# A decoder block in one list schedule: from a schedule of its first phase to a schedule of the whole program

## The chip, the cores and the metric

The kernel runs on one core of one Trainium2 chip. The metric is device time in microseconds (us) of that core. Five engines work side by side, each through its own stream of instructions in a fixed order: PE (matmuls; its weight loads are listed as PEld), DVE, ACT and POOL (elementwise work), and SP, which here only issues DMA transfers.

## The reference

One decoder block on x of 1024 tokens by 1024 features, all in float32:

```python
xn = rmsnorm(h, norm_mix_g);  proj = xn @ w_in
att = forgetting_attention(q, k, v, log_sigmoid(f + b))      # 8 heads of 64, causal
gm  = chunked_spatial_gating(gelu(u), vg, ...)               # 8 groups of 64, chunks of 128 tokens
h = h + concat(att, gm) @ w_out
xn = rmsnorm(h, norm_ffn_g)
a, g = split(conv3(xn @ w_up))                               # 2 x 2816 columns, causal conv of width 3
h = h + (silu(g) * a) @ w_down
out = rmsnorm(h, norm_final_g)
```

## The kernel before

The large products are done in float32 precision from a pair of reduced-precision terms: each operand x is split into a high part (rounded to fp32r) and a low part (x minus the high part), and a product is three matmuls, high by high, high by low, low by high. `split_w` (L387) does that for weights: ACT casts the high part (L390), DVE subtracts for the low part (L396). Around this, each large product is a Strassen-like scheme with seven block products in place of eight; POOL forms the sums of weight blocks (L1342 to L1345 for the FFN), DVE the sums of inputs.

The stages follow each other on PE: the projection (from L335 on, `tmul` L487 to L493, `product` L630 to L635, and `qk_step` L845, which makes one unit of queries and keys, split into high and low parts and written to DRAM through `emit` (L790, DMAs at L797); L887 empties the last bank of a unit into the second half of a tile `G` whose first half such a DMA is still reading); the attention, head by head (`Head`, L982: logits L1007/L1008, transposes L1028, the weighted sum of values L1047), with the spatial gating in between; w_out (`wmm`, L1362 to L1366, accumulating four groups G0 to G3 into one PSUM bank), the second norm (`norm2`, L1376 to L1386), and `flip` (L1390 to L1418), which transposes the normed tokens (L1400) and splits them into `xB`/`xT` operands; the FFN's up projection, 22 units; and the down projection (L1650) with the final norm.

One unit of the up projection (`up_a`, `up_b`, L1487 to L1565) is seven products of 12 matmuls of 128x512 each, into banks named `b` and `s`. DVE empties the banks: `u` (L1517, L1521), and `h` in parts (L1527, L1529, L1545). The last product of a unit accumulates onto the bank that L1527 reads, so it waits for L1527. Then the convolution runs on DVE (L1505 and L1507 on tiles `cg` and `ca`), the gate (L1548), and, once in two units, four sums `hs` (L1559 to L1562), which go to DRAM as `hx` and come back in the down projection as `sg`. For later units, weights are loaded (`raw<-wup`, on SP), summed by POOL into `sg`, and split by ACT and DVE into `wha` (two blocks per unit, straight from `raw`) and `whb` (five blocks).

The order is set in two ways. Class `Pace` (L33) records the instructions from `pace.start()` (L305) to `pace.settle()` (L1288), that is the projection, the attention and the gating. `settle` (L150) builds the dependencies of these, gives each a due time (backwards from PE's order: the due time of a successor less the instruction's own latency and a hop), and lets `run` (L226) issue them in a simulated machine, on each engine the ready one that is due first; the order that results is pinned on each engine. It runs up to three rounds and keeps the best. What stands in the program after L1288 (w_out, norm2, flip, the whole FFN) is not recorded. It keeps the tile framework's order, and by hand a few instructions are held behind others: `behind` (L400) holds weight splits behind the sums of `flip(7)` (key "sums") or behind a unit's L1527 (key "hg").

Of the kernel before, what the change touches and what calls it, by code (L numbers as in the profile page):

```python
# [10 lines left out]
BF16 = mybir.dt.bfloat16  # L11
# [21 lines left out]
class Pace:  # L33
# [3 lines left out]
    def __init__(self, tc):  # L37
        self.tc, self.slot, self.ring, self.prev, self.held = tc, {}, {}, {}, {}

    def keep(self, t, key):  # L40

        name = t.tensor.name if hasattr(t, "tensor") else t.name
        self.slot[name] = key
        self.prev[name] = self.held.get(key)
        self.held[key] = name

    def pool(self, p):
        pace = self

        class Paced:  # L50

            def tile(self, shape, dt, tag=None, bufs=None, name=None, **kw):
                if tag is None:
                    t = p.tile(shape, dt, name=name, **kw)
                    pace.keep(t, (id(p), name))
                    return t
                n = pace.ring.get((id(p), tag), 0)
                pace.ring[id(p), tag] = n + 1
                b = bufs or 4
                tag = "%s.%d" % (tag, n % b) if b > 1 else tag  # L60
                t = p.tile(shape, dt, tag=tag, bufs=1, name=name, **kw)
                pace.keep(t, (id(p), tag))
                return t

            def release(self):
                p.release()

        return Paced()
# [4 lines left out]
    def view(self, a):  # L73
# [6 lines left out]
        if t.name in self.slot:  # L80
            if self.slot[t.name][0] in self.banks:
                return t.name, 0, P, 1, True
# [61 lines left out]

    def psum(self, a):
        return self.slot.get(a.bass_ap.tensor.name, (0, ""))[0] in self.banks

    banks = ()

    def settle(self, rounds=3):  # L150
# [4 lines left out]
        for i in list(self.tc.nc.cur_bb.bb.instructions)[self.first:]:  # L155
# [27 lines left out]
            ops.append((i, eng, c, deps, SET.get(str(getattr(i, "func", "")).split(".")[-1], 0) if eng == "ACT" else 0))  # L183
        for name, ks in opens.items():
            old = self.prev[name]
            while old is not None and old not in uses:
                old = self.prev[old]
            for k in ks if old is not None else ():
                ops[k][3].update(uses[old] - {k})
# [1603 lines left out]
```

## Time and profile before

| what | us |
|---|---|
| median of 3 runs | 1074.82 (1074.76 to 1074.94) |
| the profiled execution, its own time | 1075.99 |
| its span in the trace | 1074.3 |
| PE busy | 1053.2 (98%) |
| DVE busy | 905.7 (84%) |
| ACT busy | 574.8 (54%) |
| POOL busy | 238.9 (22%) |

The granted TensorE clock of the profiled execution was 0.995 of full speed on average. Two kinds of time are told apart below. Busy time counts an instruction from its start to its end; matmuls overlap one another, so PE is 98% busy without being at its peak. Lost time on PE is read from the gaps between the starts of its matmuls. The rows of an answer that lists instructions in time give the start in us from the span's beginning, the duration, the engine, the line, what is written and read, and, in brackets, the idle time before it and what ended it. Tiles are named as in the program, with buffer numbers left out.

### The profile page before, as it was taken

Reading aid. Unit: us, or ns where it says so; the run is one execution under the profiler, and the core shown is the slowest. Engines: PE = TensorE matmul, PEld = TensorE weight load, DVE = VectorE, ACT = ScalarE, POOL = GpSimd, SP = SyncE. Lnnn points to the kernel's source line nnn. Section 1 sums busy time; section 2 is a strip of 40 time slices with the busy share of each in tenths; the row PEclk is TensorE's granted clock in tenths of the full one; section 3 lists DMA queues with packets and bytes.
Section 4 is the critical chain, followed back from the end, with each engine's and each line's share of the span. In section 5 each row is a group of like instructions: output and inputs, shape, how many; then the busy total and the mean of one; then the engine's idle time right before and its main releaser. Section 6 shows DMA issues by size and latency. Waiting matters only on the chain.

```text
span 1074.3 us, 14284 instructions
## 1 busy us (share of the span) xinstructions
PE 1053.2 (98%) x4885; PEld 865.8 (81%) x4885; DVE 905.7 (84%) x1390; ACT 574.8 (54%) x1006; POOL 238.9 (22%) x211
## 2 busy tenths in 40 slices
PE   9999999999999999998999999999999999999997
PEld 6888778788888877876888888888888888888886
DVE  6986699898888868999899899998998776898774
ACT  6657445577776746753444444444344444454653
POOL 0002224232362250054233232233322000000000
PEclk9999999999999999999999999999999999999999
DMA  9243336886675354223323323232331998333442
GB/s 333 96 145 98 90 115 176 265 255 189 193 220 158 109 199 164 77 73 125 120 67 119 126 82 115 99 114 83 108 118 50 302 342 305 106 92 99 144 122 96
DMA packets 64712, 158.16 MB, mean 147 GB/s; under 512 B 7672, under 2 KB 7936, under 8 KB 64640
## 3 DMA queue, kind: packets, MB, share of 16 engines
q1 hardware_dynamic: 64352, 156.70, 44.8%
q8 instruction: 38, 0.62, 0.2%
q10 hardware_dynamic: 288, 0.56, 0.1%
q14 instruction: 34, 0.28, 0.1%
HBM read 114.95 MB, written 42.27 MB: 146 GB/s over the span
## 4 chain that ended last, share of the span: by engine, by line
PE 82%; issue 7%; DVE 5%; DMA 3%; POOL 2%; ACT 1%; SPq 0%; POOLq 0%; DVEq 0%; ACTq 0%
PE s L1455 20%; PE b L1455 14%; PE s L1650 11%; PE b L1650 8%; PE s L493 6%; PE b L493 5%; PE fl L1123 4%; PE po L1047 3%; PE tr L1028 3%; PE b L635 2%; PE s L635 2%; PE lg L1008 2%; PE lg L1007 2%; DMA qd<-G 1%; DMA x<-kd 1%
## 5 line engine op out<-in xcount | busy, mean ns | idle before, releaser
L1455 PE MATMUL s<-xT,whb 128*128 128x512 f32 x804 | 189.8, 389 | 0.2 <-DVE u L1517 0.2
L1455 PEld LDWEIGHTS s<-xT,whb 128*128 128x128 f32 x804 | 150.7, 188 | 32.0 <-DVE u L1517 0.6
L1455 PE MATMUL b<-xB,wha 128*128 128x512 f32 x528 | 127.2, 390 | 2.0 <-DVE wha L396 2.0
L1650 PE MATMUL s<-whb,wha 128*128 128x512 f32 x528 | 120.2, 389 | 0.0
L1455 PEld LDWEIGHTS b<-xB,wha 128*128 128x128 f32 x528 | 98.9, 188 | 22.8 <-DVE wha L396 2.4
L1650 PEld LDWEIGHTS s<-whb,wha 128*128 128x128 f32 x528 | 99.1, 188 | 20.7
L390 ACT CAST wha<-sg 128x512 fp32r<-128x512 f32 x77 | 48.0, 623 | 97.1 <-PE b L1650 46.0
L390 ACT CAST whb<-sg 128x512 fp32r<-128x512 f32 x82 | 50.6, 618 | 74.8 <-PE s L1455 67.1
L1650 PE MATMUL b<-whb,wha 128*128 128x512 f32 x396 | 90.2, 389 | 0.0
L396 DVE TENSOR_TENSOR wha<-sg,wha 128x512 fp32r<-128x512 f32 x77 | 53.0, 690 | 41.9 <-ACT wha L390 41.9
L1650 PEld LDWEIGHTS b<-whb,wha 128*128 128x128 f32 x396 | 74.3, 188 | 15.4
L1123 PE MATMUL fl<-whl,H 128*128 128x512 f32 x192 | 71.5, 416 | 0.0
L396 DVE TENSOR_TENSOR whb<-sg,whb 128x512 fp32r<-128x512 f32 x82 | 62.8, 767 | 9.0 <-ACT whb L390 8.7
L1455 PE MATMUL s<-xB,whb 128*128 128x512 f32 x264 | 64.9, 395 | 4.6 <-DVE h L1527 4.6
L1455 PEld LDWEIGHTS s<-xB,whb 128*128 128x128 f32 x264 | 50.4, 192 | 15.6 <-DVE h L1527 5.0
L1455 PE MATMUL b<-xT,whb 128*128 128x512 f32 x252 | 61.0, 389 | 0.0
L1342 POOL TENSOR_TENSOR sg<-raw 128x512 f32<-128x512 f32 x20 | 28.1, 1404 | 146.9 <-DVE whb L396 84.0
L1047 PE MATMUL po<-pt,V 128*128 128x512 f32 (+1 forms) x192 | 58.8, 364 | 1.0 <-DVE pt L1039 1.0
L1039 DVE TENSOR_TENSOR pt<-tr,pt 128x512 fp32r<-128x512 f32 (+2 forms) x96 | 51.9, 551 | 8.6 <-ACT pt L1034 8.1
L1034 ACT CAST pt<-tr 128x512 fp32r<-128x512 f32 (+3 forms) x96 | 45.4, 475 | 25.8 <-PE tr L1028 23.1
L1455 PEld LDWEIGHTS b<-xT,whb 128*128 128x128 f32 x252 | 47.2, 188 | 10.0 <-DVE whb L396 0.3
L1343 POOL TENSOR_TENSOR sg<-sg,raw 128x512 f32<-128x512 f32 x20 | 41.2, 2058 | 62.7 <-issue 62.6
(382 smaller groups left out, 2344.1 us busy)
## 6 DMA issues: line engine op xcount, KB each, us to landing
raw<-wup SPq DMA_DIRECT2D x44, 512.0 KB, 3.6
sg<-hx SPq DMA_DIRECT2D x77, 256.0 KB, 2.6
hx<-hs SPq DMA_DIRECT2D x44, 256.0 KB, 2.2
hx<-ca SPq DMA_DIRECT2D x33, 256.0 KB, 2.0
xT<-wdn SPq DMA_DIRECT2D x28, 256.0 KB, 4.8
raw<-wqk SPq DMA_DIRECT2D x8, 512.0 KB, 3.9
qd<-G SPq DMA_DIRECT2D x16, 256.0 KB, 9.3
kd<-G SPq DMA_DIRECT2D x16, 256.0 KB, 3.2
```

Source lines behind the costliest of these rows:

```text
L390: act.copy(h, src)
L396: return eng.tensor_tensor(out=l, in0=src, in1=f32(h), op=ALU.subtract)
L493: pe.matmul(banks[m], xs(n, xi, k)[:, ms], w[:, wi, :], start=(first and k == 0 and c == 0), stop=(k == 3 and c == 2), skip_group_check=True)
L635: pe.matmul(ps, w[:, wi, ks], xs(n, xi, k), start=(first and c == 0), stop=(c == 11), skip_group_check=True)
L1028: pe.transpose(ps[:, (q - 4 * hf) * P:(q - 4 * hf + 1) * P], self.t[q][:, k * P:(k + 1) * P], ident)
L1034: act.copy(pt[:, 0, o:512], ps[:, o:512])
L1039: dve.tensor_tensor(out=pt[:, 1, o:512], in0=ps[:, o:512], in1=f32(pt[:, 0, o:512]), op=ALU.subtract)
L1047: pe.matmul(self.po[hf][:, o:512], lhs, pt[:, s, o:512], start=(k == 0 and s == 0), stop=(k == 4 * hf + 3 and s == 1), skip_group_check=True)
L1123: pe.matmul(self.bank, sgT[k][:, xi, ts_], self.w[hf, k][:, wi, :], start=(k == 0 and i == 0), stop=(k == 3 and i == 2))
L1343: pool.tensor_tensor(out=s[1], in0=s[0], in1=a11, op=ALU.add)
L1455: pe.matmul(ps, w[:, wi, ks], xb[:, xi, k, :], start=(first and n == 0), stop=(n == 11), skip_group_check=True)
L1650: pe.matmul(banks[bk + m], xh[:, xi, ms], wh[:, wi, :], start=(first and p_ == 0 and n == 0), stop=(p_ == NP - 1 and n == 2), skip_group_c ...
```

## The change

It touches what the planner sees and how it weighs, and hardly what is computed. The instructions are the same in kind and number; only their order differs.

1. `pace.settle()` moves from L1288 to the end of the program, and the pools that came after it (`upl`, `xtp`, `upr`, `pst`, `dn`) are opened through `pace.pool`. So the schedule covers w_out, norm2, flip and the FFN too. The hand-set orders (`gates`, `behind`, `after`) go.
2. A place in SBUF is no longer followed by pool and tag but by bytes: each pool knows the pool under it on its side (`extent`), and `prior` finds for each tile the earlier tiles that lay on its bytes, whichever pool they came from. A pool that opens where another was released waits for all that used the released one ("TURN", an entry without time).
3. Reads of one PSUM bank by two engines are put in order.
4. The due time: for a predecessor on the same engine (SP excepted) the successor's due time is taken less the predecessor's pace, no longer less its latency and a hop. Matmuls that accumulate into one bank, 12 of them say, so become due close together.
5. SP issues at most 3000 ns of transfer time ahead of the modelled bus (`BACKLOG`).
6. `flip` of the first four token tiles writes, per bank, ACT's high part and ACT's copy one after the other, and DVE's low parts (`lo_of`) behind them.

```diff
@@ prior: which earlier tiles lay on a tile's bytes
+    def prior(self, uses):
+        now, prev = {"sb": [], "psum": []}, {}
+        for name in self.made:
+            pool, key = self.slot[name]
+            a, b = pool.extent(key)
+            old, keep = set(), []
+            for x, y, n in now[pool.space]:
+                if x < b and a < y:
+                    old.add(n)
...
+            prev[name] = set().union(*({n} if n in uses else prev[n] for n in old))
+        return prev
@@ settle
-                        if hit and (w or o[1]):
+                        if hit and (w or o[1] or self.bank(name) and ops[o[0]][1] != eng):
...
+        for p in {p: 0 for p, _ in self.slot.values()}:
+            if p.after:
+                ops.append((None, "TURN", (0, 0, 0), set().union(*(whose[q] for q in p.after)), 0))
+                for k in whose[p]:
+                    ops[k][3].add(len(ops) - 1)
...
                 for s in succ[k]:
-                    d = min(d, due[s] - o[2][1] - HOP)
+                    d = min(d, due[s] - (o[2][0] if ops[s][1] == o[1] != "SP" else o[2][1] + HOP))
@@ run
-                f = free[e]
+                f = max(free[e], bus - BACKLOG) if e == "SP" else free[e]
@@ block_kernel
     for hf in range(2):
         wo_split(3, hf, "pool")
-    pace.settle()
...
-    upl = tc.alloc_tile_pool(name="upl", bufs=1, reuse_waits="tile")
-    xtp = tc.alloc_tile_pool(name="xtp", bufs=1, reuse_waits="tile")
+    upl = pace.pool(tc.alloc_tile_pool(name="upl", bufs=1, reuse_waits="tile"))
+    xtp = pace.pool(tc.alloc_tile_pool(name="xtp", bufs=1, reuse_waits="tile"))
...
-                behind(split_w(wr[:, ("A11", "A12").index(n), :], (t[:, 0], t[:, 1])), "sums" if i < AHEAD else "hg")
+                split_w(wr[:, ("A11", "A12").index(n), :], (t[:, 0], t[:, 1]))
...
         if tt < 4:
             for n, p3 in (("B11", pp[0]), ("B21", pp[1])):
-                hl_of(n, c, p3)
+                act.copy(XB[n][:, 0, :, c], p3)
+                act.copy(xt[n][:, :, c], p3)
             for n, p3 in (("B11", pp[0]), ("B21", pp[1])):
-                act.copy(xt[n][:, :, c], p3)
+                lo_of(n, c, p3)
...
         finish(4 + m, hi)
+    pace.settle()
     dn.release()
```

The lines of the changed kernel have shifted: L396 is L441 there, L797 is L835, L815 to L817 are L853 to L855, L960 is L998, L1505 and L1507 are L1539 and L1541, L1517 is L1551, L1521 is L1555, L1527 is L1561, L1529 is L1563, L1545 is L1575, L1548 is L1578, L1559 to L1562 are L1589 to L1592, and L1575 is L1605.

How the order moves is shown at three places. In the rows, a number after a tile's name tells its instances apart, and is the same in both kernels.

The first is on DVE, in the first units of the up projection, where the weight block `wha_834` is split that PE needs for the first product of unit 3 (`b_836`). Before:

```order
L1521 TENSOR_TENSOR u_831_4761<-u_829_4746,s_830_4748 128x512
L1507 SCALAR_TENSOR_TENSOR ca_818_4706<-h_804_4611,cp_75,ca_818_4706 128x1022
L1527 TENSOR_TENSOR h_833_4776<-u_831_4761,s_832_4763 128x512
L1548 TENSOR_TENSOR ca_818_4706<-ca_818_4706,cg_816_4685 128x1024
L396 TENSOR_TENSOR whb_835_4806<-sg_826_4739,whb_835_4806 128x512
L396 TENSOR_TENSOR whb_841_4832<-sg_827_4740,whb_841_4832 128x512
L1529 TENSOR_TENSOR h_833_4776<-u_829_4746,s_830_4748 128x512
L396 TENSOR_TENSOR wha_834_4803<-raw_823_4734,wha_834_4803 128x512
L396 TENSOR_TENSOR wha_840_4829<-raw_823_4734,wha_840_4829 128x512
```

And now:

```order
L1563 TENSOR_TENSOR h_812_4663<-u_808_4633,s_809_4635 128x512
L441 TENSOR_TENSOR whb_821_4717<-raw_731_4062,whb_821_4717 128x512
L1605 TENSOR_TENSOR h_815_4682<-b_801_4578,u_814_4681 128x512
L441 TENSOR_TENSOR wha_862_4960<-raw_851_4878,wha_862_4960 128x512
L1575 TENSOR_TENSOR h_804_4611<-s_811_4650,u_808_4633 128x512
L441 TENSOR_TENSOR wha_834_4803<-raw_823_4734,wha_834_4803 128x512
L441 TENSOR_TENSOR wha_840_4829<-raw_823_4734,wha_840_4829 128x512
L1539 SCALAR_TENSOR_TENSOR cg_816_4685<-h_812_4663,cp_75,cg_816_4685 128x1023
L1551 TENSOR_TENSOR u_829_4746<-b_822_4721,u_814_4681 128x512
L1539 SCALAR_TENSOR_TENSOR ca_818_4706<-h_804_4611,cp_75,ca_818_4706 128x1023
```

The split of `wha_834` stood behind two convolution steps (`ca_818`), a gate and the emptying of `h_833`; it now stands ahead of all of these, directly behind `h_804` and `wha_862`, a block for unit 4 that was split 25 rows further down before.

The second place is on DVE some 15 rows later, at `h_861`, the emptying of the bank `s_860` for which the last product of unit 3 waits. Before:

```order
L1548 TENSOR_TENSOR ca_842_4837<-ca_842_4837,cg_839_4825 128x1024
L1521 TENSOR_TENSOR u_859_4905<-u_857_4890,s_858_4892 128x512
L1559 TENSOR_TENSOR hs_846_4853<-ca_818_4706,ca_842_4837 128x512
L396 TENSOR_TENSOR whb_863_4963<-sg_854_4883,whb_863_4963 128x512
L1560 TENSOR_TENSOR hs_847_4854<-hs_846_4853,ca_818_4706 128x512
L1561 TENSOR_TENSOR hs_848_4855<-ca_818_4706 128x512
L396 TENSOR_TENSOR whb_869_4989<-sg_855_4884,whb_869_4989 128x512
L396 TENSOR_TENSOR whb_871_4999<-sg_853_4882,whb_871_4999 128x512
L1562 TENSOR_TENSOR hs_849_4856<-hs_847_4854,ca_842_4837 128x512
L396 TENSOR_TENSOR wha_886_5092<-raw_875_5022,wha_886_5092 128x512
L1527 TENSOR_TENSOR h_861_4933<-u_859_4905,s_860_4920 128x512
```

And now:

```order
L1578 TENSOR_TENSOR ca_818_4706<-ca_818_4706,cg_816_4685 128x1024
L1551 TENSOR_TENSOR u_857_4890<-b_850_4865,u_837_4810 128x512
L1539 SCALAR_TENSOR_TENSOR ca_842_4837<-h_815_4682,cp_75,ca_842_4837 128x1023
L1555 TENSOR_TENSOR u_859_4905<-u_857_4890,s_858_4892 128x512
L1541 SCALAR_TENSOR_TENSOR ca_842_4837<-h_815_4682,cp_75,ca_842_4837 128x1022
L441 TENSOR_TENSOR whb_863_4963<-sg_854_4883,whb_863_4963 128x512
L1563 TENSOR_TENSOR h_833_4776<-u_829_4746,s_830_4748 128x512
L441 TENSOR_TENSOR whb_869_4989<-sg_855_4884,whb_869_4989 128x512
L441 TENSOR_TENSOR wha_868_4986<-raw_851_4878,wha_868_4986 128x512
L441 TENSOR_TENSOR whb_871_4999<-sg_853_4882,whb_871_4999 128x512
L1561 TENSOR_TENSOR h_861_4933<-u_859_4905,s_860_4920 128x512
```

The four sums `hs_846` to `hs_849`, the gate of `ca_842`, and the block `wha_886` (for unit 5) stood ahead of `h_861`, as did the convolution `cg_839`; now they come behind it, and `wha_868`, a block of unit 4, comes ahead of it.

The third place is on SP in the projection, at the DMAs around the write of one unit's results to DRAM (`qd<-G`, issued twice for a tile; L887 writes into the same tile `G` and starts when this transfer has ended). The rows `x<-qd`, `x<-kd`, `x<-ncd` load what the attention's first head reads, `pt<-vd` its values, `raw<-wv` weights. Before:

```order
L824 DMA raw_177_1610<-wv 128x1024
L824 DMA raw_176_1608<-wv 128x1024
L813 DMA x1_170_1551<-qd_112 128x1024
L814 DMA x1_170_1551<-kd_113 128x1024
L797 DMA qd_112<-G1_111_999 64x2x512 x2
L815 DMA x2_171_1552<-kd_113 64x1024
L816 DMA x2_171_1552<-kd_113 64x1024
L817 DMA x2_171_1552<-ncd_115 128x1024
L960 DMA pt_187_1659<-vd_116 128x1024
L797 DMA qd_112<-G1_111_999 64x2x512 x2
```

And now:

```order
L862 DMA raw_177_1610<-wv 128x1024
L851 DMA x1_170_1551<-qd_112 128x1024
L835 DMA qd_112<-G1_111_999 64x2x512 x2
L862 DMA raw_176_1608<-wv 128x1024
L852 DMA x1_170_1551<-kd_113 128x1024
L853 DMA x2_171_1552<-kd_113 64x1024
L835 DMA qd_112<-G1_111_999 64x2x512 x2
L854 DMA x2_171_1552<-kd_113 64x1024
L855 DMA x2_171_1552<-ncd_115 128x1024
L998 DMA pt_187_1659<-vd_116 128x1024
```

The last `qd<-G` of the rows before stood behind the rest of the `x2_171` loads (L816, L817) and behind `pt_187<-vd`; now it stands ahead of these three, and the earlier `qd<-G` has one of the two `raw<-wv` loads behind it that stood in front.

More of the change, by code (lines that the diff above doesn't have):

```diff
@@ L230, in run @@
         ready = [0.0] * n
-        can = {e: [] for e in ("PE", "DVE", "ACT", "POOL", "SP")}
+        can = {e: [] for e in ("PE", "DVE", "ACT", "POOL", "SP", "TURN")}
         free = dict.fromkeys(can, 0.0)
@@ L252, in run @@
             i, e, (cad, lat, x), deps, fn = ops[k]
+            turn = e == "TURN"
             can[e].remove(k)
@@ L278, in run @@
         return order, start, end
-SLACK = 30000.0
-LOOK = {"PE": 0.0, "DVE": 0.0, "ACT": 0.0, "POOL": 0.0, "SP": 0.0}
-def after(tc, later, earlier):
-    tc.add_manual_dep(later.ins, earlier.ins.name, mybir.DependencyInfo(
-        mybir.DependencyClass.NoSync, mybir.DependencyReason.DATA), reason="order")
+SLACK, BACKLOG = 30000.0, 3000.0
+LOOK = {"PE": 0.0, "DVE": 0.0, "ACT": 0.0, "POOL": 0.0, "SP": 0.0, "TURN": 0.0}
 @with_exitstack
@@ L1469, in block_kernel @@
         if i == 0:
-            last = flip(7)
+            flip(7)
             WB[0](("S2", "S3"))
-            gates["sums"] = last
     def late_sum(n, src):
```

121 lines of the change are left out of this document (70 added, 51 removed).

## The prediction

> **What bounds the kernel now.** I read the page first, then PE's waits, a table of stretches, and the instructions in time around each wait.
>
> The page's first lines:
>
> ```profile
> span 1074.3 us, 14284 instructions
> PE 1053.2 (98%) x4885; PEld 865.8 (81%) x4885; DVE 905.7 (84%) x1390; ACT 574.8 (54%) x1006; POOL 238.9 (22%) x211
> ```
>
> PE is the bound, so the change can only remove time in which PE stands still or runs at half pace. PE's waits, longest first (engine, bank and line, what ended the wait, us, times, longest):
>
> ```profile
> PE s L1455 <- DVE h L1527: 4.6, 1, 4.6
> PE b L1455 <- DVE wha L396: 2.0, 1, 2.0
> PE s L493 <- DVE G L887: 1.9, 1, 1.9
> PE b L635 <- ACT whl L390: 1.6, 1, 1.6
> ...
> PE po L1047 <- DVE pt L1039: 1.0, 1, 1.0
> PE s L1400 <- DVE pt L1374: 0.7, 1, 0.7
> PE s L749 <- DVE gg L748: 0.5, 1, 0.5
> ```
>
> Seven waits, 12.3 us in sum. That is nearly all there is to win: the stretches (us of each engine busy, with instruction counts; then PEclk, DMA share, GB/s) show where PE keeps its pace.
>
> ```profile
> 200.00:240.00 40.00, 38.13 (x191) 31.50 (x191) 35.45 (x80) 26.46 (x54) 13.33 (x20) 0.96 0.76 242
> 440.00:480.00 40.00, 37.87 (x165) 30.49 (x164) 38.82 (x42) 23.14 (x32) 14.52 (x8) 1.00 0.25 84
> 480.00:520.00 40.00, 35.37 (x151) 28.82 (x150) 36.50 (x41) 15.73 (x22) 14.78 (x9) 0.96 0.33 114
> 520.00:840.00 320.00, 320.00 (x1413) 264.86 (x1412) 290.58 (x323) 143.68 (x202) 102.71 (x64) 1.00 0.31 104
> ```
>
> From 520 to 840 us PE starts 1413 matmuls in 320 us, one every 0.2265 us, and never stands. In 440 to 520 it starts 316, where that pace would make 353: 37 are missing, 8.4 us. The DVE column says who lags: 38.82 of 40 us in 440 to 480, against 290.58 of 320 (36.3 of 40) later. So the largest part of what can be won lies in the first units of the up projection, where DVE is full; the next in 200 to 240, where the granted clock fell to 0.96.
>
> **The change part by part.** The instructions are the same, so no busy time is added; only the order moves. Each term is the loss removed (minus) or made (plus).
>
> Term A and B, the up projection's first units. PE in time (start, us, then the idle time before the row in brackets):
>
> ```profile
> 468.31 0.61 PE L1455 MATMUL b<-xB,wha 128*128 128x512 f32 x2
> 470.89 2.57 PE L1455 MATMUL b<-xB,wha 128*128 128x512 f32 x10 [1.97 <-DVE wha L396]
> ...
> 481.46 5.60 PE L1455 MATMUL s<-xT,whb 128*128 128x512 f32 x24
> 491.69 4.34 PE L1455 MATMUL s<-xB,whb 128*128 128x512 f32 x12 [4.63 <-DVE h L1527]
> 495.87 2.90 PE L1455 MATMUL b<-xB,wha 128*128 128x512 f32 x12
> ```
>
> PE stands 1.97 us for the low part of `wha_834` and 4.63 us for `h_861`. After the second wait the 12 matmuls take 495.87 - 491.69 = 4.18 us instead of 12 x 0.2265 = 2.72: 1.46 us more at half pace. DVE in the same time:
>
> ```profile
> 455.29 0.69 DVE L396 TENSOR_TENSOR whb<-raw,whb 128x512 fp32r<-128x512 f32 x1 [0.37 <-ACT whb L390]
> ...
> 465.70 3.47 DVE L396 TENSOR_TENSOR whb<-sg,whb 128x512 fp32r<-128x512 f32 x2
> ...
> 469.69 2.85 DVE L396 TENSOR_TENSOR wha<-raw,wha 128x512 fp32r<-128x512 f32 x2
> ...
> 484.72 1.77 DVE L1561 TENSOR_TENSOR hs<-ca 128x512 f32<-128x512 f32 x1
> 486.42 1.28 DVE L396 TENSOR_TENSOR whb<-sg,whb 128x512 fp32r<-128x512 f32 x2
> 487.69 1.68 DVE L1562 TENSOR_TENSOR hs<-hs,ca 128x512 f32<-128x512 f32 x1
> 489.29 1.75 DVE L396 TENSOR_TENSOR wha<-raw,wha 128x512 fp32r<-128x512 f32 x1
> 490.96 0.68 DVE L1527 TENSOR_TENSOR h<-u,s 128x512 f32<-128x512 f32 x1
> 491.56 0.68 DVE L396 TENSOR_TENSOR whb<-raw,whb 128x512 fp32r<-128x512 f32 x1
> ...
> 495.16 1.28 DVE L1505 SCALAR_TENSOR_TENSOR cg<-h,cp,cg 128x1023 f32<-128x1023 f32 x1
> 496.35 0.68 DVE L1545 TENSOR_TENSOR h<-s,u 128x512 f32<-128x512 f32 x1
> ```
>
> By starts, a 128x512 row costs DVE 0.60 us (490.96 to 491.56) and a row twice as long 1.19 (495.16 to 496.35), and some of the short ones 1.7. The long ones stand beside POOL:
>
> ```profile
> 484.42 1.52 POOL L1342 TENSOR_TENSOR sg<-raw 128x512 f32<-128x512 f32 x1 [3.11 <-DVE whb L396]
> 487.23 1.59 POOL L1343 TENSOR_TENSOR sg<-sg,raw 128x512 f32<-128x512 f32 x1 [1.28 <-issue]
> ```
>
> Each stretched row ends 0.55 us after the POOL row does (485.94 and 486.49; 488.82 and 489.37): DVE waited for POOL's end, some 1.1 us.
>
> A: `wha_834` now comes third behind the row at 455.29, after `wha_862` and a part of `h_804`. That row ends at 455.98, so the split ends by 455.98 + 3 x 0.60 = 457.8, eleven us before PE wants it (470.89 - 1.97 = 468.9). Its inputs are there: the loads and ACT's high parts in time are
>
> ```profile
> 448.09 0.88 SPq L1317 DMA_DIRECT2D raw<-wup x2
> ```
>
> ```profile
> 453.07 1.67 ACT L390 CAST wha<-raw 128x512 fp32r<-128x512 f32 x3 [3.12 <-DMA raw<-wup]
> ```
>
> both before 455. A = -2.0, and if the cast were late there is the eleven us as cover.
>
> B: between 455.98 and `h_861` there now stand 27 rows, 20 short and 7 long: 20 x 0.60 + 7 x 1.19 = 20.3 us. For POOL I add 5.5: the rows at 465.70 and 469.69 took 3.47 and 2.85 where two short ones take 1.28, so 2.2 and 1.6 lost, and half as much again; and 1 us for waits on ACT like the 0.37. `h_861` then starts at 482.8 and ends at 483.5. PE wants it at 491.69 - 4.63 = 487.1, less A 485.1. The cover is 1.6 us: thin, two more stretched rows use it up. B = -(4.63 + 1.46) = -6.1; the other end is 0.
>
> Term C, the projection. SP, PE and DVE around 203 us:
>
> ```profile
> 190.28 0.61 SPq L817 DMA_DIRECT2D x<-ncd x1
> 191.40 0.33 SPq L960 DMA_DIRECT2D pt<-vd x1
> 192.68 2.31 SPq L797 DMA_DIRECT2D qd<-G x2
> ```
>
> ```profile
> 203.16 0.69 DVE L887 TENSOR_TENSOR G<-s,pt 128x512 f32<-128x512 f32 x1 [1.47 <-DMA qd<-G]
> ```
>
> ```profile
> 203.91 4.61 PE L493 MATMUL s<-whl,x 128*128 128x512 f32 x12 [1.87 <-DVE G L887]
> 208.35 0.40 PE L927 MATMUL b<-H,wy 128*128 128x512 f32 x1
> ```
>
> The write issued at 192.68 lets L887 go at 203.16, 10.5 us later. It now stands ahead of L816, L817 and a `vd` load, 1.28 MB by their shapes; at the 242 GB/s of 200 to 240 us these take 5.3 us, and issue moves up by about 1.3 (from 192.68 to 191.4). L887 is wanted 1.9 us sooner, so the wait should go with 3 us to spare; these loads land later, but they are for the attention, which begins past this stage. The 12 matmuls took 208.35 - 203.91 = 4.44 us instead of 2.72, so the term is 1.87 + 1.72 = 3.6 at most. PE's own order moves too here, and the DMA engines stay full, so I take -3.0; the other end is 0.
>
> The Trainium skill, TensorE: Matmul & The Clock Gate, "What's actually happening", says that the clock halves after an idle window of about 3.4 us, and that the windows run freely. By an idle window of 3.4 us the 1.87 us of idling could not have cost the 1.72, and C would be worth 1.9 instead of 3.6; the trace shows the slow 12 matmuls directly behind that wait, so the row decides.
>
> Term D, the transposes of `flip` that wait 0.7 for DVE (L1374): PE's last w_out matmuls of the first banks come about 14 matmuls earlier, DVE's first norm follows: -0.7, other end 0.
>
> Term E, the 0.5 at L749 and 1.6 at L635 in the projection. The first goes, as four more matmuls (0.9 us) stand ahead of it; the second hangs on a chain through POOL and DVE in unchanged order, and PE arrives earlier by what the first gave: 0.
>
> Term F, the 1.0 at L1047 (`pt`): a convert of a gate row that waits for a DMA comes ahead of `pt` on DVE: +0.2, ends -1.0 and +1.5.
>
> Term G, the price of A and B. What `h_861` overtakes is not gone: the four `hs`, the `ca_842` gate, the `cg_839` convolution and `wha_886` are 5 short and 3 long rows, 6.6 us, up to 8 when stretched, against 1.2 for `wha_862` and `wha_868` brought forward. DVE gives it back out of its slack, 320 - 290.58 = 29.4 us in 320, 1.75 us in a unit of 84 matmuls (19.0 us): some four units in which it runs late. What is late next is the same reading of banks (L1527) and splits; +1.5, ends 0 and +10.
>
> The down projection moves rows on SP and DVE only, where PE never waited before: 0, ends -0.3 and +1.
>
> Sum: -2.0 - 6.1 - 3.0 - 0.7 + 0 + 0.2 + 1.5 + 0 = -10.1. The profiled execution took 1075.99 and would take 1065.9; the median of the runs shown is 1.17 us below that execution (0.1%), so I predict 1064.7.
>
> **The rivals.**
>
> Rival 1: one of the two large terms stays. Without C it is 1067.7; without B, because the 1.6 us of cover is used up by POOL, 1070.8. For it: the thin cover, and the DMA engines at 0.76 in 200 to 240. Against: both orders move the right row by several us.
>
> Rival 2, slower: DVE's late work. In each of the next five units the last product waits for `h` as it did once at 491.69. Half of that wait, 2.3 us, five times, and the half pace of 1.46 in two of them, is 14.4 us against gains of 11.6 (without G): +2.8, 1077.6. It decides from 2.3 us per unit. For it: DVE at 36.3 of 40 us busy, and rows that grow from 0.68 to 1.77 when POOL runs. Against: from 520 us on PE waits for nothing in spite of that, and the planner's order puts `h` early.
>
> The Trainium skill, SBUF — State Buffer, "SBUF: two separate sides", speaks against the change here: it calls the port shared by DVE and GpSimd an exclusive lock, which a DVE operation with two SBUF inputs loses for the whole of a GpSimd operation. The trace agrees (DVE ends 0.55 us behind POOL both times); by this rule every row that B lets slide towards POOL's sums can grow by 1.1 us, which is the mechanism of rival 2.
>
> Rival 3, no change: the wait is DVE's work and not its order. DVE was full from 440 to 508, and a reordering of full work only moves the wait to another row; with C given back at the chain of term E, the sum is within 2 us of zero: 1073 to 1076. Against: part of that work was not wanted for another 10 us and more.
>
> Rival 4, better: all listed waits go and G is nothing, with half of E and F: -2.0 - 6.1 - 3.6 - 0.7 - 1.0 - 0.5 = -13.9, 1060.9.
>
> **How the numbers follow.** A measurement of this kernel can tell about 0.2% from no change, 2.15 us: faster is below 1072.7, slower above 1077.0. The forecast (1062.5 to 1066.9, the sum with D, F and G moved by 2.2 in all) has a chance of 0.43, rival 1 0.26, rival 4 and better 0.09, rival 3 0.11, rival 2 0.11. Faster: 0.43 + 0.26 + 0.09 and none of the others, 0.78; same 0.11; slower 0.11. Range: rivals 1 and 4 with the forecast are 0.78; to hold 0.8 it runs from 1060.5 to 1072.8, where the upper end takes in a rival 1 with 2 us of G more.
>
> **What would show it.** In the profile of the changed kernel: no wait of PE for `wha` and for `h` before 520 us, PE with 176 or more matmuls in each 40 us from 440 on, and a granted clock of 1.00 there; L887 not behind the `qd<-G` transfer; L635's wait still there, perhaps longer. DVE should show less idle time from 490 to 600 than before. Wrong would be: waits of PE for L1561 in units 4 to 9 (rival 2), a wait at L887 as long as before (C), or the whole gain lost at a new row of the list of waits.

## The result and the profile after

The changed kernel takes 1063.33 us (median of 4 runs, 1063.08 to 1064.09), beside 1074.79 us for the kernel before on the same chip: 11.5 us less, ratio 0.9897 with a 95% interval of 0.988 to 0.9914. The profiled execution took 1063.19 us, 12.8 us less than that of before.

The page's first lines, and all of PE's waits (each engine has the same number of instructions as before; the 60 fewer of the first line are of kinds that are not counted as busy):

```profile
span 1061.5 us, 14224 instructions
PE 1050.1 (99%) x4885; PEld 866.2 (82%) x4885; DVE 914.1 (86%) x1390; ACT 574.6 (54%) x1006; POOL 245.3 (23%) x211
```

```profile
PE s L405 <- DVE one L406: 1.3, 1, 1.3
PE s L531 <- DVE G L925: 0.9, 1, 0.9
PE s L1435 <- DVE xn L1417: 0.6, 1, 0.6
PE s L673 <- DVE wy L441: 0.6, 1, 0.6
PE s L787 <- DVE gg L786: 0.5, 1, 0.5
PE s L673 <- DVE G L892: 0.3, 1, 0.3
```

The two long waits for `h` (4.6) and `wha` (2.0) are gone. L925 (L887 of before) is still waited for, 0.9 instead of 1.9. The stretches, in the columns of before:

```profile
200.00:240.00 40.00, 40.00 (x215) 33.80 (x216) 37.24 (x86) 29.03 (x60) 12.74 (x20) 1.00 0.80 256
440.00:480.00 40.00, 40.00 (x177) 32.88 (x176) 39.79 (x46) 19.42 (x29) 17.89 (x10) 1.00 0.29 99
480.00:520.00 40.00, 40.00 (x178) 33.10 (x178) 39.01 (x44) 19.01 (x26) 13.97 (x9) 1.00 0.33 113
520.00:840.00 320.00, 320.00 (x1413) 264.97 (x1412) 302.52 (x327) 145.46 (x203) 108.48 (x63) 1.00 0.35 116
```

In 440 to 520 us PE starts 355 matmuls instead of 316, its full pace, with the clock at 1.00. DVE pays for it in the open: it is busy 39.79 and 39.01 of 40 us, and from 520 to 840 us 302.52 of 320 instead of 290.58. Four more instructions fall into that stretch. Of the others some take less time than before, and others more, the `wha` splits above all; here they are before and after the change (520 to 720 us; count, us in sum, mean ns):

```profile
L396 DVE TENSOR_TENSOR wha<-raw,wha 128x512 fp32r<-128x512 f32 x20 | 13.6, 681 | 0.0
```

```profile
L441 DVE TENSOR_TENSOR wha<-raw,wha 128x512 fp32r<-128x512 f32 x23 | 26.7, 1160 | 0.0
```

They take longer because 12 of the 23 are now held up by a POOL operation that ran when they started, and before none was (the last section has the counts). PE waits for none of it. DVE at the two places of the prediction, and PE behind the second:

```profile
451.06 0.68 DVE L441 TENSOR_TENSOR wha<-raw,wha 128x512 fp32r<-128x512 f32 x1
...
452.26 1.28 DVE L441 TENSOR_TENSOR wha<-raw,wha 128x512 fp32r<-128x512 f32 x2
...
478.63 0.68 DVE L1561 TENSOR_TENSOR h<-u,s 128x512 f32<-128x512 f32 x1
```

```profile
480.29 2.88 PE L1490 MATMUL s<-xB,whb 128*128 128x512 f32 x12
```

`wha_834` is the first of the two at 452.26. `h_861` ends at 479.31, 1.0 us before PE begins the product that needs it: the cover of 1.6 us was foreseen thin and is thinner.

### The profile page after: what moved, and what is told of

Same layout as the page of the kernel before. It is cut to its first block, busy times and chain, and to the rows that moved or that the text cites. A ratio compares the mean times of both kernels' runs of the same rounds, so it can differ in the third digit from the quotient of the medians.

```text
span 1061.5 us, 14224 instructions
## 1 busy us (share of the span) xinstructions
PE 1050.1 (99%) x4885; PEld 866.2 (82%) x4885; DVE 914.1 (86%) x1390; ACT 574.6 (54%) x1006; POOL 245.3 (23%) x211
## 4 chain that ended last, share of the span: by engine, by line
PE 93%; DVE 4%; DMA 2%; issue 0%; SPq 0%; ACT 0%; DVEq 0%
PE s L1490 23%; PE b L1490 17%; PE s L1678 11%; PE b L1678 8%; PE s L531 6%; PE b L531 5%; PE fl L1161 4%; PE po L1085 3%; PE tr L1066 3%; PE b L673 2%; PE lg L1046 2%; PE lg L1045 2%; PE s L673 2%; DMA qd<-G 1%; PE s L756 1%; PE b L1401 1%
## 5 line engine op out<-in xcount | busy, mean ns | idle before, releaser
L1490 PE MATMUL s<-xT,whb 128*128 128x512 f32 x804 | 189.4, 389 | 0.0
L1490 PEld LDWEIGHTS s<-xT,whb 128*128 128x128 f32 x804 | 150.8, 188 | 31.6 <-DVE whb L441 0.3
L1490 PE MATMUL b<-xB,wha 128*128 128x512 f32 x528 | 126.7, 389 | 0.0
L1490 PEld LDWEIGHTS b<-xB,wha 128*128 128x128 f32 x528 | 99.0, 188 | 20.5
L441 DVE TENSOR_TENSOR wha<-sg,wha 128x512 fp32r<-128x512 f32 x77 | 53.0, 688 | 40.9 <-ACT wha L435 40.9
L1379 POOL TENSOR_TENSOR sg<-raw,raw 128x512 f32<-128x512 f32 x20 | 41.4, 2072 | 143.5 <-DVE whb L441 143.5
L1490 PE MATMUL s<-xB,whb 128*128 128x512 f32 x264 | 63.4, 389 | 0.0
L441 DVE TENSOR_TENSOR whb<-sg,whb 128x512 fp32r<-128x512 f32 x82 | 61.4, 759 | 2.0 <-ACT whb L435 2.0
L1161 PE MATMUL fl<-whl,H 128*128 128x512 f32 x192 | 62.4, 406 | 0.0
L1490 PE MATMUL b<-xT,whb 128*128 128x512 f32 x252 | 60.7, 389 | 0.0
L1072 ACT CAST pt<-tr 128x512 fp32r<-128x512 f32 (+2 forms) x96 | 45.5, 474 | 26.1 <-PE tr L1066 20.3
L1490 PEld LDWEIGHTS s<-xB,whb 128*128 128x128 f32 x264 | 49.5, 188 | 10.3
L1077 DVE TENSOR_TENSOR pt<-tr,pt 128x512 fp32r<-128x512 f32 (+1 forms) x96 | 51.7, 550 | 6.6 <-ACT pt L1072 6.0
L1490 PEld LDWEIGHTS b<-xT,whb 128*128 128x128 f32 x252 | 47.3, 188 | 9.8
L1377 POOL TENSOR_TENSOR sg<-raw 128x512 f32<-128x512 f32 x20 | 36.3, 1814 | 81.8 <-DMA raw<-wup 61.6
L1085 PE MATMUL po<-pt,V 128*128 128x512 f32 (+1 forms) x192 | 49.0, 349 | 0.0
```

What stands on the lines that cost most here:

```text
L441: return eng.tensor_tensor(out=l, in0=src, in1=f32(h), op=ALU.subtract)
L1072: act.copy(pt[:, 0, o:512], ps[:, o:512])
L1077: dve.tensor_tensor(out=pt[:, 1, o:512], in0=ps[:, o:512], in1=f32(pt[:, 0, o:512]), op=ALU.subtract)
L1085: pe.matmul(self.po[hf][:, o:512], lhs, pt[:, s, o:512], start=(k == 0 and s == 0), stop=(k == 4 * hf + 3 and s == 1), skip_group_check=True)
L1161: pe.matmul(self.bank, sgT[k][:, xi, ts_], self.w[hf, k][:, wi, :], start=(k == 0 and i == 0), stop=(k == 3 and i == 2))
L1377: pool.tensor_tensor(out=s[0], in0=a21, in1=a22, op=ALU.add)
```

## The experiments

Times of kernels made from the one before stand beside that kernel on the same chip. A kernel made from the changed one has its ratio to the kernel before, to be set against 0.9897. Where its time is set against 1063.33 us, the two come from different chips (on which the kernel before took 1074.79 to 1075.43), so the difference by the ratios stands in brackets beside it. A row of waits is from one profiled execution of each.

Edits that add lines shift those behind them, by up to 24 in the first two kernels: L1514 and L1459 there and below are L1490 of the changed kernel or L1455 of the kernel before, L1585 is L1561, and the names of the tiles tell the rest. Half pace of PE is read from its starts; in the traces it goes with a granted clock of 0.5.

**Which stretch of the order matters.** Two kernels put the order of before back into a part of the changed kernel, on all five engines at once. The first does it for the first units of the up projection.

```diff
+        one = closed(was["DVE"][:613] + was["PE"][:2153])
+        two = closed(was["DVE"][:675] + was["PE"][:2489]) | one
+        for e, v in was.items():
+            q = best[1][e]
+            mid = [k for k in v if k in two and k not in one]
+            best[1][e] = [k for k in q if k in one] + mid + [k for k in q if k not in two]
```

(`was` is the order of before; `closed` adds all that an instruction depends on.)

> The changed kernel with the first four units of the up projection (from the emptying of u_808 to about the bank s_884) in the order that they had before, on all five engines; all else, w_out, norm and flips included, keeps the changed order. Theory O (the order inside the up projection took the waits away): both waits come back in full, 9.0 us, 1072. Theory H (DVE is full there, and what helped is that DVE comes out of the flips earlier; the order inside counts for little): 2 us or less, 1065.5. A mixture shows as a part of the 9.0.

Measured: 1075.74 us, ratio to before 1.0008 (0.9998 to 1.0019): the whole gain is gone. PE's longest waits, and two stretches:

```profile
PE s L1514 <- DVE h L1585: 4.8, 1, 4.8
PE s L1514 <- DVE xT L1445: 1.8, 1, 1.8
...
PE b L1514 <- DVE wha L465: 1.1, 1, 1.1
PE s L1514 <- ACT xT L1448: 1.1, 1, 1.1
```

```profile
440.00:480.00 40.00, 38.83 (x164) 31.18 (x162) 36.51 (x41) 20.70 (x30) 14.65 (x8) 0.96 0.22 79
480.00:520.00 40.00, 35.24 (x149) 28.64 (x148) 29.86 (x37) 13.85 (x21) 13.69 (x9) 0.96 0.29 94
```

The wait for `h` is back in its full size, that for `wha` in half, and 313 matmuls start in these 80 us, three fewer than before the change. The two waits for `xT` stand at the seam (437 and 439 us), where PE's old order meets the new flips; they are of the experiment's making, and so is a part of the loss: in 400 to 440 us PE starts 188 matmuls instead of the changed kernel's 201, which is 2.9 us. In 440 to 520 us it starts 42 fewer, 9.5 us, where theory O named 9.0. So the old order inside is enough to bring the waits back, as theory O says. Theory H is not answered, because the head start that it needs was lost at the seam: the `whb` row of DVE that starts at 455.29 before (the prediction shows it), and at 449.86 in the changed kernel, starts at 454.99 here.

The second kernel does the same for w_out, norm2, flips and late sums (DVE from 537 to 613, PE from 1815 to 2153).

> The changed kernel with w_out, the second norm, the flips and the late sums (some 380 to 445 us) in the order of before, on all engines; the up projection keeps the changed order. Theory O: only the small gain of term D is lost, +0.5 to +1, 1064. Theory H: the head start is lost, DVE is behind from 445 us on, and PE waits in the first units again: +6 or more, 1069.5.

Measured: 1085.81 us, ratio 1.0098 (1.0081 to 1.0116), 22 us more than the changed kernel.

```profile
PE b L1423 <- ACT G L459: 4.0, 1, 4.0
PE s L1459 <- DVE xn L1441: 3.7, 2, 1.9
PE s L1514 <- DVE u L1579: 2.3, 1, 2.3
PE s L1514 <- DVE xT L1445: 1.8, 1, 1.8
```

```profile
440.00:480.00 40.00, 34.14 (x148) 27.37 (x149) 36.98 (x48) 21.74 (x33) 9.09 (x6) 0.96 0.22 79
480.00:520.00 40.00, 40.00 (x179) 33.10 (x178) 39.12 (x42) 19.78 (x28) 20.59 (x12) 1.00 0.28 99
```

Some 12 us lie at the front seam, before 400 us (the 4.0 for `G` at 383 us is the start of w_out, which before was woven into the attention), and say nothing. In 440 to 480 us PE starts 148 matmuls instead of 177, and waits for `xn`, `xT` and `u`, that is for the flips and the first unit's operands. That is some 10 us more, as theory H had it (+6 or more, with waits in the first units), and not +1 at most. But it can't be put down to the old order of the flips alone, for in the kernel before PE waits only 0.7 us in them; the seam ahead of them has its part. Behind them, from 480 us on, the new order of the up projection runs at full pace, and neither the wait for `wha` nor that for `h` comes back (though PE, held up ahead of it, gave DVE time). So for these two waits the run agrees with theory O. How much of the gain the new order of the flips holds stays open.

**Nine rows by hand.** The kernel before, with nine DVE rows moved, most of those whose new places the text above names; the rest is left to the framework.

```diff
+        if i == 5:
+            for q in sums4 + lows[4]:
+                after(tc, q, held[0])
+            for q in slow:
+                after(tc, q, lows[2][0])
```

(`sums4`: hs_846 to hs_849; `lows`: the low parts of `wha` by unit; `held`: h_861; `slow`: the steps of ca_818.)

> The kernel before with one engine's order changed in the first units of the up projection: the convolution and gate of ca_818 stand behind the low part of wha_834, and the four sums hs_846 to hs_849 and wha_886, wha_892 behind h_861; the other four engines keep their order row for row. Theory (the waits are a matter of order; DVE's late work fits into its later slack): both waits of 1.97 and 4.63 us and the 1.46 us at half pace go, -8.1 us, 1066.7. Rival (DVE is full, so the wait only moves to another row): -3 us or less, 1071.8 or more, with new waits of PE for DVE between 440 and 560 us.

Measured: 1072.96 beside 1075.42 us, ratio 0.9976 (0.9966 to 0.9987): 2.5 us of the 8.1. PE's waits in the up projection, PE at the first, and DVE ahead of it:

```profile
PE b L1459 <- DVE wha L396: 2.5, 1, 2.5
...
PE s L1459 <- DVE u L1526: 1.5, 2, 0.8
```

```profile
469.75 4.15 PE L1459 MATMUL b<-xB,wha 128*128 128x512 f32 x10 [2.45 <-DVE wha L396]
473.73 2.89 PE L1459 MATMUL b<-xT,whb 128*128 128x512 f32 x12
```

```profile
461.80 1.12 DVE L396 TENSOR_TENSOR whb<-sg,whb 128x512 fp32r<-128x512 f32 x1 [1.94 <-ACT whb L390]
...
463.44 2.88 DVE L396 TENSOR_TENSOR whb<-sg,whb 128x512 fp32r<-128x512 f32 x2
466.25 1.77 DVE L396 TENSOR_TENSOR whb<-raw,whb 128x512 fp32r<-128x512 f32 x1
...
468.54 1.16 DVE L396 TENSOR_TENSOR wha<-raw,wha 128x512 fp32r<-128x512 f32 x1
```

The wait for `h` is gone as foreseen, with the half pace behind it (-4.6 and -1.5). But into the place that the convolution left, the framework drew two `whb` splits forward, so that four stand ahead of `wha_834`; the first of the four waits 1.94 for ACT, whose order was left alone. So PE's wait for `wha` grew by 0.5, and half pace now follows it: its ten matmuls take 3.98 us, in the kernel before 2.41 (470.89 to 473.30), 1.6 more. With 1.3 more for `u` this makes -2.7, beside the 2.5 measured. The theory held for one move and was not tried by the other. The rival had the size and the sentence, that the wait moves to another row; that it moves because DVE is full is not shown, as the rows that came in its place were the framework's choice.

**The hand-set order.** The kernel before, with `behind` doing nothing.

```diff
-        if key in gates:
+        if False:
```

> The kernel before without the hand-set order of the weight splits (behind does nothing); PE's order stays row for row. On DVE wha_834 then comes ahead of the convolutions of the first unit, but the four sums still stand ahead of h_861. Theory (each wait is set by its own row): the 1.97 goes; of the 4.63 only the 1.75 of wha_886 that no longer stands ahead; -2.0 - 1.7 = -3.7, 1071.1, and the half pace may stay. Rival (the hand-set order was needed: splits taken early push the sums of the last flips back): slower than before by 1 us or more.

Measured: 1075.24 beside 1075.42, ratio 0.9996 (0.9986 to 1.0007): no change. The wait for `wha` is gone from PE's list, as expected, but that for `h` is 4.7 as before, and waits of 0.7 for `u` (L1521) and 0.5 for ACT (L1494) are new. The two stretches:

```profile
440.00:480.00 40.00, 39.37 (x172) 31.65 (x171) 39.82 (x43) 22.58 (x33) 14.72 (x8) 1.00 0.25 86
480.00:520.00 40.00, 34.52 (x143) 27.79 (x142) 36.01 (x40) 15.63 (x21) 13.16 (x9) 0.91 0.31 112
```

Seven more matmuls start in the first and eight fewer in the second, 315 in all as against 316. The expected 3.7 us failed. Of the 2.0 that the wait for `wha` gave, the two new waits take 1.0 net, and half pace behind the wait for `h` 0.6 more than before (the 12 matmuls take 4.79 us, 489.71 to 494.50). The wait for `h` did not shrink by the 1.75 of `wha_886`, because two other `wha` splits now stand ahead of it (at 476.57 and 485.31, where before one did). The reading that fits is that on a DVE that is full (39.82 of 40 us) two waits close behind one another are one debt and not two terms: what the first gives the second takes.

**The due times.** The old rule in the changed kernel, and the new rule in the kernel before (whose schedule ends after the gating).

```diff
-                    d = min(d, due[s] - (o[2][0] if ops[s][1] == o[1] != "SP" else o[2][1] + HOP))
+                    d = min(d, due[s] - o[2][1] - HOP)
```

> The changed kernel with the due times of before (successor's due time less latency and a hop for all). Theory (the scope of the schedule makes the gain of the up projection, the due times that before 400 us): no wait of PE between 440 and 520 us, and the losses before 400 us come back: +3.5 us on the changed kernel, 1066.8. Rival (the due times do it all): 1071 or more, with waits in 440 to 520 us. Second rival (the due times do nothing): within 1 us of 1063.3.

> The kernel before, its schedule still ending after the gating, with the new due times alone. Theory (the due times make the gain of the projection and the attention, the scope of the schedule that of the up projection): the losses of PE before 400 us fall as in the changed kernel, about -3.5 us, 1071.3, and the waits of 1.97 and 4.63 us stay. Rival (the due times only bundle matmuls and change no wait): within 1 us of before.

Measured: 1067.36 us, ratio 0.9918 (0.9906 to 0.993), for the old rule in the changed kernel, 4.0 us more than that (2.3 by the ratios, whose intervals overlap); and 1075.47 beside 1075.42, ratio 1.0 (0.999 to 1.0011), for the new rule in the old kernel. With the old rule PE's waits are

```profile
PE b L531 <- ACT V L481: 1.7, 1, 1.7
PE b L673 <- ACT whl L435: 1.6, 1, 1.6
PE s L531 <- DVE G L925: 1.5, 1, 1.5
...
PE s L1490 <- DVE h L1561: 0.8, 1, 0.8
```

None but the 0.8 lies in the FFN, and that is at its end, past 840 us. So the whole scope takes the waits of 440 to 520 us away without the new due times. What the due times add lies before 400 us (the 1.7 for `V`, the 1.6 for `whl`, and 0.6 more for `G`), and its worth, 2 to 4 us, is not clear of the noise. In the kernel before they do take the waits for `whl` and `G` down (to 0.7 in two parts and to 0.5), and yet the time is unchanged: the expectation of -3.5 failed, within 1 us was right. In the profiled execution a wait for `V` grew from 0.4 to 1.4, so that PE's waits fell by 2.4 us in sum, and 1.7 of this went into half pace: the stretch at 204 us is gone, but there is one at 121 us, and that behind the wait for `h` lasts twice as long (granted clock 0.91 in 480 to 520 us, before 0.96).

**The write that L887 waits for.** One move on SP, made in the kernel before and undone in the changed one.

```diff
+        q = best[1]["SP"]
+        q[at - 2:at + 3] = q[at + 1:at + 3] + q[at - 2:at + 1]
```

(`at` is the place of the first `vd` load; the other kernel has the reverse.)

> The kernel before with one move on SP: the second pair of qd writes (the one issued at 192.68) stands ahead of L816, L817 and the first vd load. Theory (the transfer ends late because of what is queued in front): it is issued by 191.5 and done by about 200.5, L887 is no longer late, and 1.87 + 1.72 = 3.6 us go: 1071.2. Rival (the DMA engines are full, and the loads that now come behind are waited for as well, or PE waits for something else there): -1 us or less, or slower.

> The changed kernel with one move on SP undone: the second pair of qd writes again behind L854, L855 (L816, L817 of before) and the first vd load. Theory (what is queued in front sets the wait): L925 waits some 3 us longer, PE's wait of 0.92 becomes about 4 with half pace behind it: +3 to +5 us, 1066.3 to 1068.3. Rival (the loads queued in front do not matter, PE's other order took the wait away): within 1 us of 1063.3.

Measured: in the kernel before, 1074.28 beside 1075.42, ratio 0.999 (0.998 to 0.9999): 1.1 us of 3.6. In the changed kernel, 1070.12, ratio 0.9951 (0.9937 to 0.9965), 6.8 us more (5.8 by the ratios) instead of 3 to 5. There L925 (now L928) waits 5.30 us for the transfer, and PE, at L531 (now L534), for L925:

```profile
208.33 3.35 PE L534 MATMUL s<-whl,x 128*128 128x512 f32 x7 [5.47 <-DVE G L928]
```

So in the changed kernel what stands ahead of this write on SP's queue does set the wait. In the kernel before the theory's first link failed: the write stands ahead in the queue and yet is issued at 192.80, no sooner than before (192.68), as SP waits 2.3 us for DVE first. L887 (there L890) runs at 202.98 instead of 203.16, with no idle time before it, so it no longer waits for the transfer, but comes hardly sooner:

```profile
202.98 0.67 DVE L890 TENSOR_TENSOR G<-s,pt 128x512 f32<-128x512 f32 x1
```

PE's wait shrank from 1.87 to 0.26 because PE came 1.4 us later (203.45 instead of 202.04). Half pace now followed another wait of PE, one that was there all along:

```profile
159.55 0.73 PE L638 MATMUL b<-H,whl 128*128 128x512 f32 x2 [1.60 <-ACT whl L393]
...
161.23 3.66 PE L638 MATMUL b<-H,whl 128*128 128x512 f32 x10
164.73 0.62 PE L638 MATMUL s<-x,wy 128*128 128x512 f32 x2
```

The ten matmuls take 3.50 us; in the kernel before, behind the same wait of 1.60, they took 2.26:

```profile
161.05 2.43 PE L635 MATMUL b<-H,whl 128*128 128x512 f32 x10
163.31 0.62 PE L635 MATMUL s<-x,wy 128*128 128x512 f32 x2
```

So this profile does not show that the 1.1 us come from the write's place. Half pace follows a wait of 1.6 us in one execution and not in another. The prediction booked its 1.72 us to this one wait as if it were sure.

**The limit on SP.** BACKLOG is the part of the change that moved this pair.

```diff
-SLACK, BACKLOG = 30000.0, 3000.0
+SLACK, BACKLOG = 30000.0, 1e9
```

> The changed kernel with no limit on what SP may issue ahead (BACKLOG 1e9 ns). The second pair of qd writes then stands behind L854, L855 and the first vd load, as before the change. Theory (BACKLOG is the part of the change that moved this pair): PE's wait at L925 grows to some 4 to 5.5 us as in the run with that one move undone, +4 to +7 us. Rival (DVE's and PE's order move with it, so that the wait is smaller): +0 to +3.

Measured: 1071.0, ratio 0.9953 (0.9936 to 0.9971), 7.7 us more than the changed kernel (6.0 by the ratios). The size is about as the theory said and the place is not:

```profile
PE s L1678 <- ACT wha L435: 2.1, 1, 2.1
...
PE b L1678 <- ACT wha L435: 1.2, 1, 1.2
...
PE s L531 <- DVE G L925: 0.9, 1, 0.9
```

The pair does stand behind the three loads again (issued at 194.69, behind the `vd` load at 193.12), and L925 runs 5.9 us later than in the changed kernel, at 205.09. But L925 is waited for as long as there, because PE's order moved too: PE does 18 more matmuls first and comes at 204.91 instead of 198.97, as the rival said. So the write's place sets the wait only for a given order of PE. The new waits are at the head of the down projection (871 to 893 us), where SP now issues the `wdn` loads in blocks of 8 to 16 and the `hx` writes and `sg` loads of the last units come behind them:

```profile
860.00:900.00 40.00, 36.15 (x158) 28.93 (x157) 27.30 (x45) 17.43 (x32) 0.00 (x0) 1.00 0.81 292
```

That is 158 matmuls in 40 us, where PE's pace makes 177: 4.3 us. A stretch of half clock at 122 us, which the changed kernel's profile doesn't have, is 1.7 of the rest. The theory fell: BACKLOG did move this pair, but the greater part of what the limit is worth lies where the whole-program schedule reaches SP's queue for the first time, a place that the kernel before, without planning it, did not lose at.

**How much late work DVE can carry.** One and two more DVE operations of 128x1024 in each of ten units.

```diff
         conv(hg, cg, NFF + i)
+        for _ in range(2 if 3 <= i < 13 else 0):
+            dve.tensor_tensor(out=hg, in0=hg, in1=hg, op=ALU.mult)
```

> The changed kernel with one more DVE operation of 128x1024 in each of ten units of the up projection (units 3 to 12, counted from 0): a tile that is no longer read is multiplied by itself, about 1.2 us, 12 us in sum, more beside POOL. Theory (DVE's late work is paid from slack; from 520 to 840 us the changed kernel's DVE is busy 302.52 of 320 us, so about 1.0 us per unit is left): nearly all is covered, +0 to +3 us. Rival (the up projection is at the edge, rival 2 of the prediction): each operation shows in full, +10 us or more.

> The same with two such operations in each of the ten units, 24 us in sum. Theory: 10 to 17 us of it are covered by slack (29.4 us in 320 of before at most), the rest shows: +7 to +14 us, with PE waiting for L1561 and for weight splits. Rival (order hides any amount as long as DVE isn't busy all the time): +0 to +3 us. Rival (each shows in full): +22 us or more.

Measured: 1064.56, ratio 0.9905 (0.9889 to 0.992), for one, and 1066.71, ratio 0.9915 (0.9902 to 0.9929), for two: 1.2 and 3.4 us (0.9 and 1.9 by the ratios) for 12 and 24 us of work. For two,

```profile
520.00:840.00 320.00, 319.65 (x1411) 264.31 (x1410) 315.49 (x330) 141.64 (x198) 114.64 (x61) 1.00 0.29 102
```

DVE is busy 315.49 of 320 us and PE misses two matmuls. Most of the 3.4 us lies in the projection, where the planner's order changed with it: a new wait of 1.5 for `whl`, and half clock behind it from 194 to 198 us. The expected 7 to 14 us failed, and the rival that order hides the work so long as DVE has any time left fits (the planner sees the extra work and orders around it). The debt is carried through the units and paid in the down projection: in 860 to 900 us DVE is busy 34.88 of 40 us, in the changed kernel 26.51.

**flip.** As before, in the changed kernel.

```diff
-                act.copy(XB[n][:, 0, :, c], p3)
-                act.copy(xt[n][:, :, c], p3)
-            for n, p3 in (("B11", pp[0]), ("B21", pp[1])):
-                lo_of(n, c, p3)
+                hl_of(n, c, p3)
+            for n, p3 in (("B11", pp[0]), ("B21", pp[1])):
+                act.copy(xt[n][:, :, c], p3)
```

> The changed kernel with flip written as before (per bank ACT's high part and DVE's low part, then ACT's copies). Theory (a small help in 400 to 440 us alone): +0 to +1 us, and nothing beyond 440 us. Rival (banks are held longer, the flips stretch and DVE comes late into the up projection): +3 us or more with waits after 440 us.

Measured: 1064.59, ratio 0.9894 (0.9875 to 0.9914): the same as the changed kernel, as the theory had it. Its one wait in the flips is 1.3 instead of 0.6; none comes after 440 us.

## Why the prediction was right, and where it was not

The direction, the place and the size came out: 1064.7 us forecast, 1063.33 measured, 11.5 us less where 10.1 were forecast. Between the profiled executions it is 12.8 us, and the waits account for it, with 10.0 and 3.2: PE's fell from 14.2 us in sum to 4.2 (the prediction's list of seven leaves out 1.3 for `one`, 0.4 for `V` and 0.2 for `u`), and the 3.2 us that the prediction read off two stretches of half pace are gone. Rival 3, that the wait is DVE's work and not its order, is answered by the same two profiles: DVE is as full as before in 440 to 520 us, 78.8 of 80 us after 75.3, and the waits are gone.

- **A and B, -8.1.** Right in size: 39 more matmuls in 80 us are 8.8 us. Right in mechanism: the old order there brings the waits back (`a_up_back`), and the rows bear the working out. DVE takes 27.6 us for the 27 rows ahead of `h_861` (451.06 to 478.63), where 26.8 were worked out; the 33 rows that stood there before took 35.0 (455.98 to 490.96). So `h_861` comes 7.4 us sooner after the same point, and PE wanted it 6.6 sooner. The working held the start fixed, and both sides moved alike: in the changed kernel DVE starts these rows 4.9 us sooner, and PE wants `h_861` 4.8 sooner than the 485.1 worked out; 4.0 of that are the gains before 440 us (12.8 in all less 8.8). Two things stay open: whether the order of the flips is needed too, and how little of the order would do, for the rows moved by hand gave 2.5 us with the framework's order around them (`b_moves`).
- **C, -3.0.** The size is near (0.95 of the wait and the 1.72 of half pace, 2.7), and not as it was worked out. SP, DVE and PE there, in the changed kernel:

```profile
190.33 1.29 SPq L835 DMA_DIRECT2D qd<-G  x2
```

```profile
199.15 0.69 DVE L925 TENSOR_TENSOR G<-s,pt 128x512 f32<-128x512 f32 x1 [0.38 <-DMA qd<-G]
```

```profile
199.89 1.89 PE L531 MATMUL s<-whl,x 128*128 128x512 f32 x7 [0.92 <-DVE G L925]
```

  The step that failed is "the wait should go with 3 us to spare" (by its own numbers, 5.3 + 1.3 - 1.9, it would be 4.7). The prediction took the whole 5.3 us of the three loads off the write's time, but it fell only from 10.5 to 8.8 us (190.33 to 199.15); with an issue 2.4 us sooner, L925 runs 4.0 us sooner instead of 6.6. And it held PE's arrival fixed, but PE, which has 12 fewer matmuls ahead of this place, arrives 3.1 us sooner (198.97 instead of 202.04). So 0.92 of the 1.87 stays. The half pace behind it went (clock 1.00 in 200 to 240), but `b_sp_pair` shows that it is not tied to one wait, so that this part is luck.
- **D, -0.7.** Most of the wait stayed: 0.6 at L1435 for `xn`, instead of 0.7.
- **E, 0.** The two halves the other way round: the 0.5 for `gg` is still there, and the 1.6 at L635 fell to 0.6 (for `wy`) and 0.3 (for `G`), -0.7; `a_old_due` has the 1.6 again, so it is the due times.
- **F, +0.2.** The 1.0 for `pt` is gone, -1.0, its lower end.
- **G, +1.5.** Nothing: PE waits nowhere after 440 us. DVE's debt is real (302.52 against 290.58 us), but the slack is larger than the 1.75 us a unit by which it was priced, as the doses show: late work can be handed on to the down projection. Rival 2, its extreme, is answered by the same runs: 24 us of extra work cost 3.4 at most.
- **The down projection, 0.** Right for the change as it is, but on account of BACKLOG, which the prediction did not weigh there: without it, 4.3 us are lost at its head (`a_no_backlog`).

Of the Trainium skill: "SBUF: two separate sides" is borne out in its mechanism (of the DVE rows that started beside a running POOL operation, nearly all with both inputs in SBUF ended 0.55 us behind it, as the last section counts), and its price on PE was nil. "What's actually happening" on TensorE: Matmul & The Clock Gate says that windows run freely; the two traces of the wait of 1.60 us, once with half pace behind it and once without, agree with that, and disagree with an idle time of 3.4 us as the condition.

## What to carry to other kernels

A wait's row in the profile tells what came last, and moving that row alone may hand the wait to the next one: before pricing a reordering, ask how late the lagging engine is as a whole, and when the other engine will then arrive. On an engine that is full for a hundred us but not for the whole program, an order by due times over several stages can be worth several times what single moves are. When a queue of transfers comes under a planner, limit what it may issue ahead, and look for the loss where the loads of the next stage begin.

## What the runs showed of the hardware

- After idle times of PE of 1.6 to 5.5 us its matmuls ran at half pace for a while, or did not: with 1.60 us once yes (10 matmuls in 3.50 us, `b_sp_pair`) and once no (2.26, before), and with 1.97 us not (before). In the traces, but for the program's end, the clock is halved for 3.41 us at a time, or for twice that (204.4 to 207.8 and 491.1 to 494.5 us before; 489.3 to 496.1 in `b_new_due`). With two kernels at equal work, one such stretch is a difference of 1.2 to 1.7 us.
- A DVE row that starts while a POOL operation runs is held until it ends, if both its inputs are in SBUF. In 520 to 840 us, of the rows of 128x512 that started so, all 32 before and 46 of 48 now ended 0.55 us behind a POOL operation. None was held up that reads a PSUM bank (24 and 16), nor any that started first (16 and 25). That is how the `wha` splits between 520 and 720 us went from 681 to 1160 ns in the mean, only by standing elsewhere in the order.
